# A decoder layer on one core: the norm weights loaded apart from the other vectors, with an earlier exp and a shorter warm-up

## The chip, the cores and the metric

The kernel runs on one core of a Trainium2 chip. The metric is the device time of one execution in microseconds (us). The engines are TensorE (PE; its weight loads are shown apart as PEld), VectorE (DVE), ScalarE (ACT), GpSimd (POOL) and SyncE (SP), which here issues most of the DMA transfers. Each engine works through its own instructions in order and waits on semaphores for the others.

## The reference

One layer (DEPTH 1) of a hybrid decoder, batch 1, 512 tokens with 16 learned meta tokens ahead of them (528 positions), model width 1024, all float32:

```python
def rmsnorm(x, w):
    xf = xf * lax.rsqrt(jnp.mean(xf * xf, axis=-1, keepdims=True) + EPS)
    return xf.astype(x.dtype) * w

h = jnp.concatenate([meta, x], axis=1)
u = rmsnorm(h, mix_norm_w[i])
proj = u @ w_in[i]                 # u_pool, z, xbc, dt_raw, gates
...
y_pool = pool_mixer(u_pool, ...) @ w_pool_up[i]
y_ssd = mamba2_branch(z, xbc, dt_raw, conv_w, conv_b, dt_bias, a_log, ...) @ w_ssd_out[i]
h = h + (gate_pool * y_pool + gate_ssd * y_ssd) @ w_o[i]
v = rmsnorm(h, mlp_norm_w[i])
hid = jax.nn.relu(v @ w_ff1[i])
h = h + (hid * hid) @ w_ff2[i]
out = rmsnorm(h, final_norm_w)
```

Only the start matters here: x is scaled by mix_norm_w and multiplied with columns of w_in. The division by the root mean square is done later, on the products, since it is one factor per token. dt = softplus(dt_raw + dt_bias) and a = -exp(a_log) feed the state-space branch.

## The kernel before, in words

Every float32 product is made of three matmuls on operands split into a high and a low part: ScalarE rounds the operand to the array's format (xh, whi), VectorE subtracts to get the rest (xl, wlo), and TensorE sums high by high, low by high and high by low. The model width is the contraction, in eight slices of 128 (k = 0 to 7). x arrives transposed, one slice a transfer (xt), 128 partitions by 528 tokens.

The start works as follows.

- Constants: an identity, ones in two formats (ones_f, and ones_r for the matmuls), eps. A table vs of 128 by 234 holds all small vectors of the layer, one column each: columns 0 to 7 are the norm weights (V_MIX), further ones are biases, the convolution's taps, dt_bias and a_log. It is loaded in one transfer on ScalarE's queue.
- Warm-up: WARM matmuls of ones_r by ones_r into a bank that is overwritten later (line 195).
- For each slice k, x_split makes xh and xl (lines 202 and 203), scaled by the norm weight of the slice; block_split makes whi and wlo of the weights (lines 79 and 80); bc_step(k) multiplies both weight blocks wB and wC with the slice (lines 148, 149 and 151, twelve matmuls a slice, into px). The weights of the first two blocks are loaded in parts: two quarters, and a half at k = 4.
- The square of each slice is taken on ScalarE (lines 231 and 234) and summed on VectorE into q (line 235).
- After slices 3 and 7, dt_step multiplies x with the 32 columns of dt (wdt, line 211, into pdt). Then pdt is copied (dtp, line 253) and gathered by small matmuls (pdv, line 257); q is summed over partitions (pn, line 274), which gives the norm factor rsb; dt's softplus and running sum follow (lines 307 to 341), with ea = exp(a_log) from line 312.

After that come the projections of the first group, seven further groups, the pool branch, the merge and the MLP.

The order on each engine is not the order of the code: a scheduler that plans with its own costs sets it before the run, and an instruction may move ahead of others of its engine. Hardware DMA semaphores are taken in turn from eight, so a DMA also waits for the one eight places before it. The line numbers in the profile of before are those of the old kernel.

Of the kernel before, what the change touches and what calls it, by code (L numbers as in the profile page):

```python
# [9 lines left out]
F32 = mybir.dt.float32  # L10
F32R = mybir.dt.float32r
AF = mybir.ActivationFunctionType
ALU = mybir.AluOpType

P = 128
# [5 lines left out]
NK = D // P  # L21
# [13 lines left out]
V_MIX, V_BG, V_PS, V_CW, V_CB, V_DS, V_SN, V_MN, V_DTB, V_AL = (  # L35
    0, 8, 24, 32, 160, 192, 208, 224, 232, 233)
# [6 lines left out]
MERGE = (0, 4, 1, 5, 2, 6, 3, 7)  # L43

WO_ORDER = [(q, i) for q in ("b11", "b12", "b22") for i in range(2)]
WARM = 9


@with_exitstack
def kernel(ctx: ExitStack, tc, xT, x, w, vec, fnw, out):  # L50
    nc = tc.nc
    act, dve, pe, pool = nc.scalar, nc.vector, nc.tensor, nc.gpsimd

    const = ctx.enter_context(tc.tile_pool(name="const", bufs=1, side="left"))
# [8 lines left out]
    def block_tiles():  # L63
        b = nblk[0]
        nblk[0] += 1
        return (b, wp.tile([P, 1024], F32, tag="raw", name=f"raw{b}", bufs=3),
                wp.tile([P, 1024], F32R, tag="whi", name=f"whi{b}"),
                wp.tile([P, 1024], F32R, tag="wlo", name=f"wlo{b}"))

    def block_load(t, c):  # L70
        nc.sync.dma_start(t[1][:, c], w[t[0], :, c])

    def block_part(t, c):
        block_load(t, c)
        block_split(t, c)

    def block_split(t, c):
        b, raw, hi, lo = t
        act.copy(hi[:, c], raw[:, c])  # L79
        dve.tensor_tensor(lo[:, c], raw[:, c], hi[:, c].bitcast(F32), op=ALU.subtract)  # L80
# [21 lines left out]
    make_identity(nc, ident)  # L102
    ones_r = const.tile([P, P], F32R, name="ones_r")
    ones_f = const.tile([P, P], F32, name="ones_f")
    dve.memset(ones_f, 1.0)
    dve.tensor_copy(ones_r, ones_f)
    tri = const.tile([P, P], F32, name="tri")
    pool.affine_select(out=tri, in_=ones_f, compare_op=ALU.is_ge, fill=0.0, base=0,
                       pattern=[[1, P]], channel_multiplier=-1)
# [2 lines left out]
    dve.tensor_copy(sel[:, 1, :], ident[:, NM - 1 : NM].to_broadcast([P, P]))  # L112
    eps = const.tile([P, 1], F32, name="eps")
    dve.memset(eps, EPS)
    vs = const.tile([P, V_N], F32, name="vs")
    nc.scalar.dma_start(vs, vec)

    def col(off, i, n=P):
        return vs[:n, off + i : off + i + 1]
# [24 lines left out]
    def proj_step(outs, k, wblk, rhs):  # L144

        wh, wl = (t[:, k * P : (k + 1) * P] for t in wblk)
        for o, c in outs:
            pe.matmul(o, wh, rhs[0][k][:, c], start=k == 0, stop=False)  # L148
            pe.matmul(o, wh, rhs[1][k][:, c], start=False, stop=False)  # L149
        for o, c in outs:  # L150
            pe.matmul(o, wl, rhs[0][k][:, c], start=False, stop=k == NK - 1)  # L151
# [16 lines left out]
    pre = pre_stack.enter_context(tc.tile_pool(name="pre", bufs=1, side="right"))  # L168
    xt = [pre.tile([P, L], F32, name=f"xt{k}") for k in range(NK)]

    xh = [pre.tile([P, 64 + SEQ], F32R, name=f"xh{k}")[:, 64 - NM :] for k in range(NK)]
    xl = [pre.tile([P, 64 + SEQ], F32R, name=f"xl{k}")[:, 64 - NM :] for k in range(NK)]
    pre.tile([P, 24], F32, name="x_pad")
    rsb = pre.tile([P, L], F32, name="rsb")
    q = pre.tile([P, L], F32, name="q")
    X, U = (xh, xl), (uh, ul)
    H = HEADS

# [7 lines left out]
    nblk[0] += 1  # L186
    wdt = pre.tile([P, NK, H], F32, name="wdt")
    wB, wC = block_tiles(), block_tiles()
    e32 = pre.tile([P, 2 * H], F32, name="e32")[:, :H]
    dve.tensor_tensor(e32, ident[:, :H], ident[:, H : 2 * H], op=ALU.add)  # L190
    for c in (2, 3):
        dve.tensor_tensor(e32, e32, ident[:, c * H : (c + 1) * H], op=ALU.add)

    for n in range(WARM):
        pe.matmul(pdt[1].rearrange("p (a b) -> p a b", a=4), ones_r,
                  ones_r.unsqueeze(1).to_broadcast([P, 4, P]), start=True, stop=True)

    def x_load(k):
        nc.sync.dma_start(xt[k], xT[:, k, :])

    def x_split(k):
        act.activation(xh[k], xt[k], AF.Copy, scale=col(V_MIX, k))
        dve.scalar_tensor_tensor(xl[k], xt[k], col(V_MIX, k), xh[k].bitcast(F32),
                                 op0=ALU.mult, op1=ALU.subtract)

    def dt_step(kb):

        for i, run in enumerate(HF):
            for c in range(4):
                k = kb + c  # L210
                pe.matmul(pdt[i][c * H : (c + 1) * H, :HALF], wdt[:, k, :], xt[k][:, run],
                          start=kb == 0, stop=kb == 4, skip_group_check=True)

    def bc_step(k):
        proj_step(runsB, k, wB[2:], X)
        proj_step(runsC, k, wC[2:], X)

    x_load(0)
    x_split(0)
    for t in (wB, wC):  # L220
        block_part(t, slice(0, 256))
    x_load(1)
    bc_step(0)
    x_split(1)
    x_load(2)
    for t in (wB, wC):
        block_part(t, slice(256, 512))
    bc_step(1)
    def square(k):
        if k == 0:  # L230
            act.activation(q, xt[k], AF.Square)
        else:
            s = pre.tile([P, L], F32, tag="sq", name=f"sq{k}", bufs=2)
            act.activation(s, xt[k], AF.Square)
            dve.tensor_tensor(q, q, s, op=ALU.add)

    for k in range(2, NK):
        if k > 2:
            x_load(k)
        x_split(k)  # L240
        if k == 2:
            nc.sync.dma_start(wdt.rearrange("p k h -> p (k h)"), w[b, :, : NK * H])
            dve.tensor_tensor(wdt, wdt, vs[:, V_MIX : V_MIX + NK].unsqueeze(2).to_broadcast([P, NK, H]), op=ALU.mult)
        if k == 4:
            for t in (wB, wC):
                block_part(t, slice(512, 1024))
        bc_step(k)
        if k % 4 == 3:
            dt_step(k - 3)
        square(k - 2)  # L250
# [506 lines left out]
    first = []  # L757
# [478 lines left out]
```

## Time and profile before

| | us |
|---|---|
| three runs, median | 1019.76 |
| lowest, highest | 1019.51, 1020.25 |
| the profiled execution, its own time | 1019.61 |
| its span, first to last instruction | 1017.6 |

| engine | busy us | share of the span |
|---|---|---|
| TensorE matmul | 1009.4 | 99% |
| TensorE weight load | 871.3 | 86% |
| VectorE | 739.5 | 73% |
| ScalarE | 550.4 | 54% |

A row of the timeline gives the start, the duration, the engine, the line, the operation, the tiles written and read, the shape and the count; in brackets stands the idle time of the engine ahead of it and what ended it. Matmuls are pipelined, so their durations overlap; their rate is read from one start to the next. Rows of neighbouring instructions of one kind are merged, with the count at the end. The profile leaves numbers out of names: wlo is any of the low weight blocks.

### The profile page before, as it was taken

What the parts mean: (1) busy time and instruction counts of PE and PEld (TensorE: products, weight loads), DVE (VectorE), ACT (ScalarE), POOL (GpSimd) and SP (SyncE); (2) the same over time, 40 slices, a digit from 0 to 9 for tenths busy, and PEclk for the clock granted to TensorE, in tenths of its full rate; (3) what the DMA queues carried; (4) which work ended last, traced back from release to release, by engine and by line L of the source; (5) the groups of instructions that cost most, each with busy time, mean ns of one, the idle gap of its engine ahead of it and who ended that gap; (6) DMA issues with size and microseconds to landing.
All of it is one profiled execution on the core that took longest, in us unless ns stands there. A gap on an engine that the chain in (4) does not pass through costs nothing.

```text
span 1017.6 us, 14071 instructions
## 1 busy us (share of the span) xinstructions
PE 1009.4 (99%) x5697; PEld 871.3 (86%) x5697; DVE 739.5 (73%) x988; ACT 550.4 (54%) x729; POOL 10.0 (1%) x24
## 2 busy tenths in 40 slices
PE   9999999999999999999999999999999999999997
PEld 8889989999879998988899888888888888888886
DVE  7988786777736577878765557986676686776866
ACT  8774959496727339473244233475445455454444
POOL 0000000000000000000000001000000000000000
PEclk9999999999999999999999999999999999999999
DMA  7242141515223230514532334133333324334112
GB/s 248 82 163 86 40 154 33 167 24 164 82 90 119 104 104 22 166 37 133 188 100 84 109 96 150 57 116 132 104 89 114 108 83 122 92 98 125 42 42 83
DMA packets 29712, 105.62 MB, mean 104 GB/s; under 512 B 3344, under 2 KB 4688, under 8 KB 28624
## 3 DMA queue, kind: packets, MB, share of 16 engines
q1 hardware_dynamic: 26928, 92.75, 29.0%
q0 software_dynamic: 2000, 11.08, 3.1%
q8 instruction: 45, 0.74, 0.3%
q10 hardware_dynamic: 720, 0.91, 0.2%
q14 instruction: 19, 0.16, 0.1%
HBM read 102.55 MB, written 2.16 MB: 103 GB/s over the span
## 4 chain that ended last, share of the span: by engine, by line
PE 98%; DVE 1%; DMA 0%; ACT 0%; SPq 0%; issue 0%; ACTq 0%
PE px L148 6%; PE px L151 6%; PE px L149 6%; PE pf L98 6%; PE pf L96 6%; PE pf L97 6%; PE alpha L985 3%; PE alpha L987 3%; PE alpha L986 3%; PE pz L149 3%; PE pz L148 3%; PE pz L151 3%; PE py L499 2%; PE pso L96 2%; PE pp L148 2%; PE pp L151 2%
## 5 line engine op out<-in xcount | busy, mean ns | idle before, releaser
L79 ACT CAST whi<-raw 128x1024 fp32r<-128x1024 f32 (+1 forms) x134 | 136.0, 1024 | 231.1 <-PE pf L97 58.7
L80 DVE TENSOR_TENSOR wlo<-raw,whi 128x1024 fp32r<-128x1024 f32 (+1 forms) x134 | 158.8, 1188 | 120.6 <-ACT whi L79 120.6
L148 PE MATMUL px<-uh,whi 128*128 128x264 f32 (+1 forms) x448 | 120.7, 290 | 0.7 <-DVE ct L363 0.7
L149 PE MATMUL px<-ul,whi 128*128 128x264 f32 (+1 forms) x448 | 117.9, 284 | 0.0
L96 PE MATMUL pf<-vh,whi 128*128 128x512 f32 x256 | 99.8, 390 | 0.0
L98 PE MATMUL pf<-vh,wlo 128*128 128x512 f32 x256 | 99.6, 389 | 0.0
L97 PE MATMUL pf<-vl,whi 128*128 128x512 f32 x256 | 99.6, 389 | 0.0
L151 PE MATMUL px<-uh,wlo 128*128 128x264 f32 (+1 forms) x448 | 91.0, 284 | 0.0
L148 PEld LDWEIGHTS px<-uh,whi 128*128 128x128 f32 x448 | 84.7, 189 | 2.7 <-issue 2.4
L149 PEld LDWEIGHTS px<-ul,whi 128*128 128x128 f32 x448 | 84.4, 188 | 0.4 <-issue 0.2
L151 PEld LDWEIGHTS px<-uh,wlo 128*128 128x128 f32 x448 | 68.9, 188 | 0.3 <-issue 0.2
L747 DVE TENSOR_TENSOR slo<-b,shi 128x1024 fp32r<-128x1024 f32 x35 | 42.7, 1219 | 31.6 <-ACT shi L746 31.6
L746 ACT CAST shi<-b 128x1024 fp32r<-128x1024 f32 x35 | 36.8, 1051 | 51.9 <-PE pf L97 36.5
L97 PEld LDWEIGHTS pf<-vl,whi 128*128 128x128 f32 x256 | 48.1, 188 | 10.0
L98 PEld LDWEIGHTS pf<-vh,wlo 128*128 128x128 f32 x256 | 48.0, 188 | 10.0
L96 PEld LDWEIGHTS pf<-vh,whi 128*128 128x128 f32 x256 | 48.1, 188 | 9.9
L985 PE MATMUL alpha<-shi,hh 128*128 128x512 f32 x140 | 54.6, 390 | 0.0
L986 PE MATMUL alpha<-slo,hh 128*128 128x512 f32 x140 | 54.5, 389 | 0.0
L987 PE MATMUL alpha<-shi,hl 128*128 128x512 f32 x140 | 54.5, 389 | 0.0
L812 DVE TENSOR_TENSOR ht<-ht,alpha 128x1024 f32<-128x1024 f32 x35 | 42.5, 1215 | 6.1 <-PE alpha L987 6.1
L148 PE MATMUL pz<-uh,whi 128*128 128x512 f32 x112 | 43.6, 390 | 0.0
L151 PE MATMUL pz<-uh,wlo 128*128 128x512 f32 x112 | 43.6, 390 | 0.0
(409 smaller groups left out, 2431.5 us busy)
## 6 DMA issues: line engine op xcount, KB each, us to landing
raw<-in_w SPq DMA_DIRECT2D x128, 512.0 KB, 3.6
b<-in_w SPq DMA_DIRECT2D x28, 512.0 KB, 3.6
abc<-acs_d POOLq DMA_DIRECT2D x8, 1024.0 KB, 6.9
wob<-in_w SPq DMA_DIRECT2D x8, 512.0 KB, 4.6
xt<-in_xT SPq DMA_DIRECT2D x8, 264.0 KB, 4.5
ht<-in_x POOLq DMA_DIRECT2D x4, 512.0 KB, 6.5
w<-in_w SPq DMA_DIRECT2D x4, 512.0 KB, 3.5
out_dram<-out SPq DMA_DIRECT2D x4, 320.0 KB, 2.4
```

Source lines behind the costliest of these rows:

```text
L79: act.copy(hi[:, c], raw[:, c])
L80: dve.tensor_tensor(lo[:, c], raw[:, c], hi[:, c].bitcast(F32), op=ALU.subtract)
L96: pe.matmul(ps, ah, bh, start=first, stop=False)
L97: pe.matmul(ps, ah, bl, start=False, stop=False)
L98: pe.matmul(ps, al, bh, start=False, stop=last)
L148: pe.matmul(o, wh, rhs[0][k][:, c], start=k == 0, stop=False)
L149: pe.matmul(o, wh, rhs[1][k][:, c], start=False, stop=False)
L151: pe.matmul(o, wl, rhs[0][k][:, c], start=False, stop=k == NK - 1)
L747: dve.tensor_tensor(lo, src, hi.bitcast(F32), op=ALU.subtract)
L985: pe.matmul(ps[t], a[0], wh[:, cs], start=f, stop=False, skip_group_check=True)
L986: pe.matmul(ps[t], a[0], wl[:, cs], start=False, stop=False, skip_group_check=True)
L987: pe.matmul(ps[t], a[1], wh[:, cs], start=False, stop=l, skip_group_check=True)
```

## The change

There are five edits. The eight norm weight columns get a tile of their own, vm, loaded on ScalarE's queue in place of the whole table; the x split and wdt's scaling read vm. The whole table vs is loaded from SP's queue, behind the weights' last parts at k = 4. An Exp of one column of eps is issued at the start, into a tile that nobody reads. ones_r is filled by a memset in place of a copy from ones_f. WARM goes from 9 to 8. (The width of e32's tile only keeps the addresses behind vm where they were.)

```diff
-WARM = 9
+WARM = 8
...
+    dve.memset(ones_r.bitcast(F32), 1.0)
     dve.memset(ones_f, 1.0)
-    dve.tensor_copy(ones_r, ones_f)
...
     dve.memset(eps, EPS)
+
+    act.activation(const.tile([P, 64], F32, name="first")[:, :1], eps, AF.Exp)
     vs = const.tile([P, V_N], F32, name="vs")
-    nc.scalar.dma_start(vs, vec)
...
+    vm = pre.tile([P, NK], F32, name="vm")
+    nc.scalar.dma_start(vm, vec[:, V_MIX : V_MIX + NK])
...
-    e32 = pre.tile([P, 2 * H], F32, name="e32")[:, :H]
+    e32 = pre.tile([P, 56], F32, name="e32")[:, :H]
...
     def x_split(k):
-        act.activation(xh[k], xt[k], AF.Copy, scale=col(V_MIX, k))
-        dve.scalar_tensor_tensor(xl[k], xt[k], col(V_MIX, k), xh[k].bitcast(F32),
+        act.activation(xh[k], xt[k], AF.Copy, scale=vm[:, k : k + 1])
+        dve.scalar_tensor_tensor(xl[k], xt[k], vm[:, k : k + 1], xh[k].bitcast(F32),
                                  op0=ALU.mult, op1=ALU.subtract)
...
-            dve.tensor_tensor(wdt, wdt, vs[:, V_MIX : V_MIX + NK].unsqueeze(2).to_broadcast([P, NK, H]), op=ALU.mult)
+            dve.tensor_tensor(wdt, wdt, vm.unsqueeze(2).to_broadcast([P, NK, H]), op=ALU.mult)
         if k == 4:
             for t in (wB, wC):
                 block_part(t, slice(512, 1024))
+            nc.sync.dma_start(vs, vec)
```

The scheduler's order changes with it on TensorE, VectorE and ScalarE, up to TensorE's 252nd entry of some 4,840; behind that the orders are the same. On VectorE the first sum into q moves from behind xl3 to ahead of xl2, and the second and third move from behind wlo and xl5 to ahead of xl4 and xl5. On ScalarE each square follows its split more closely, and ea moves from the first place to behind the fifth square. On TensorE one matmul of slices 1, 3 and 5 and some of the pdt matmuls move ahead of the first that needs xl, and pdv and pn move ahead of five matmuls of the next projection.

## The prediction

> **What bounds the kernel now.** I read the page's busy times and chain first, then busy time by stage, then the start instruction by instruction.
>
> ```profile
> PE 1009.4 (99%) x5697; PEld 871.3 (86%) x5697; DVE 739.5 (73%) x988; ACT 550.4 (54%) x729; POOL 10.0 (1%) x24
> PE 98%; DVE 1%; DMA 0%; ACT 0%; SPq 0%; issue 0%; ACTq 0%
> 3.00:4.00 1.00, 1.00 (x4) 0.81 (x3) 0.00 (x0) 0.00 (x0) 0.00 (x0) 1.00 1.09 362
> 8.00:20.00 12.00, 12.00 (x107) 10.88 (x111) 12.00 (x24) 11.86 (x21) 0.00 (x0) 1.00 0.74 272
> 50.00:1009.00 959.00, 958.06 (x5341) 826.74 (x5340) 692.83 (x892) 509.92 (x665) 6.88 (x13) 1.00 0.32 100
> ```
>
> The first two lines are from the page; the others are stretches (width, then busy PE, PEld, DVE, ACT, POOL, then clock, DMA share, GB/s). TensorE is the bound: from 50 to 1009 us it is busy 958.06 of 959.00 us. The instruction order of the changed kernel differs from the old one only in its first 252 TensorE entries (some 50 us) and is the same behind them. So what the change is worth is how much earlier TensorE leaves the start. There, between 8 and 20 us, VectorE (12.00 of 12.00) and ScalarE (11.86) are as full as TensorE: a second limit.
>
> The start, by the timeline (start, duration, engine):
>
> ```profile
> 1.50 4.21 PE L195 MATMUL pdt<-ones_r 128*128 128x512 f32 x9 [1.50 <-DVE ones_r L106]
> 5.57 0.89 PE L148 MATMUL px<-xh,whi 128*128 128x264 f32 x2
> 6.26 0.42 PE L149 MATMUL px<-xl,whi 128*128 128x264 f32 x1
> 6.48 0.34 PE L148 MATMUL px<-xh,whi 128*128 128x264 f32 x1
> 6.66 0.28 PE L149 MATMUL px<-xl,whi 128*128 128x264 f32 x1
> 6.78 0.40 PE L151 MATMUL px<-xh,wlo 128*128 128x264 f32 x2
> 7.62 0.28 PE L148 MATMUL px<-xh,whi 128*128 128x264 f32 x1
> 7.99 0.39 PE L149 MATMUL px<-xl,whi 128*128 128x264 f32 x1
> ```
>
> Nine warm-up matmuls fill 1.50 to 5.5 us, real work starts at 5.57, and TensorE then waits between 7.62 and 7.99 for the second slice's low half.
>
> ```profile
> 1.25 1.28 ACT L312 ACT_TABLE_LOAD   x1 [1.25 <-PEq L1228]
> 4.40 0.20 ACT L312 ACTIVATE ea<-vs 128x1 f32<-128x1 f32 x1 [1.86 <-DMA vs<-in_vec]
> 4.51 0.72 ACT L202 ACTIVATE xh<-xt,vs 128x528 fp32r<-128x528 f32 x1
> 5.13 0.69 ACT L79 CAST whi<-raw 128x256 fp32r<-128x256 f32 x2
> 6.40 1.44 ACT L202 ACTIVATE xh<-xt,vs 128x528 fp32r<-128x528 f32 x2 [0.57 <-DMA xt<-in_xT]
> vs<-in_vec ACTq DMA_DIRECT2D x1, 117.0 KB, 3.6
> xt<-in_xT SPq DMA_DIRECT2D x1, 264.0 KB, 3.3
> out_dram<-out ACTq DMA_DIRECT2D x4, 192.0 KB, 2.6
> SPq L242 <- DMA vs<-in_vec: 0.3, 1, 0.3
> ```
>
> The next to last three are DMA issues, with KB and us to landing (the xt row is that of slice 0 alone); the last is SP's wait ahead of wdt. Both loads are issued at 0.81: slice 0 is there at 0.81 + 3.3 = 4.11, vs at 0.81 + 3.6 = 4.41. ScalarE waits for vs, does ea, and only at 4.51 the first split. For slice 1 it waits for slice 1's own landing, 6.40.
>
> **The change part by part.**
>
> *The eight columns alone.* The first split no longer stands behind 117 KB and ea. vm carries 4 KB on ScalarE's queue. No load of 32 bytes per partition is in the trace; the nearest rows bound its landing: 2.6 us (the output stores) and 3.6 (vs itself), so 3.4 to 4.4 us. Slice 0 is needed too (4.11), so the first split starts between 4.11 and 4.42; I take 4.15, as few bytes go with it. The row behind it, whi, follows 0.62 later, and TensorE's first real matmul 0.44 after that: 5.2 instead of 5.57, a gain of 0.36 (bounds 0.09 to 0.40).
>
> The Trainium skill's page "DMA: Bandwidth & Descriptors", Specifications, speaks against this part: below 512 B per transfer it expects less than line rate. No run here has such a load; it is one of the rivals below.
>
> *Room on the DMA engines.* The row from 3 to 4 us shows them full (1.09). Without vs, 113 KB at that row's 362 GB/s, 0.31 us of traffic goes from ahead of slice 1. wdt's issue on SP also waited 0.3 us for vs; it will wait for vm, and less. Slice 1, and with it the split at 6.40, comes 0 to 0.35 earlier; I take 0.2.
>
> *vs behind the fourth weights.* It costs SP one issue (0.43 us) ahead of slices 5 to 7 and the next weights.
>
> ```profile
> 7.09 1.28 SPq L199 DMA_DIRECT2D xt<-in_xT  x3
> DMA to landing us min/median/max: 3.3/4.5/5.3
> 8.89 0.63 ACT L234 ACTIVATE sq<-xt 128x528 f32<-128x528 f32 x1
> 9.43 1.35 ACT L202 ACTIVATE xh<-xt,vs 128x528 fp32r<-128x528 f32 x2
> 10.68 0.60 ACT L79 CAST whi<-raw 128x512 fp32r<-128x512 f32 x1
> 0.90 0.17 DVE L105 MEMSET ones_f<- 128x128 f32 x1 [0.90 <-PEq L1228]
> ```
>
> vs goes out at about 7.09 and lands near 11.6 (the eight slices' median of 4.5), at worst at 12.4 (their slowest); slice 5, one issue later, at 12.8 at worst. ea now stands on ScalarE behind the fifth square, and xh5 behind ea. Adding up ScalarE's new order from 6.20 (xh 0.67, square 0.54, weight casts 0.35 and 0.60) gives ea at 12.9 and xh5 from 13.05 to 13.75: both loads are there. Next is late only if vs lands so late that xh5 ends after 14.4, where xl5 starts (below): beyond 13.5. vs's other readers come after 25 us. Cost: nothing.
>
> *Early exp.* The table load stands at 1.25 already; "first" keeps it there and takes 0.20 us of a 1.86 us wait. Nothing. ea's own 0.11 moves off the first split and is counted above.
>
> *Ones and warm-up.* The memset of ones_r at 0.90 takes the place of memset, memset and copy: TensorE's first warm-up moves from 1.50 to about 1.1. Eight at 0.43 end near 4.7, half a microsecond before real work. No engine waits for them; what they hold is the clock (a rival).
>
> *The order that follows.* The scheduler has put the squares' sums earlier on VectorE: one more sum (q) stands ahead of xl3, and one more again, net one, ahead of xl5. This is the price of the change.
>
> ```profile
> 5.26 0.77 DVE L203 SCALAR_TENSOR_TENSOR xl<-xt,vs,xh 128x528 fp32r<-128x528 f32 x1 [3.81 <-ACT xh L202]
> 7.17 1.47 DVE L203 SCALAR_TENSOR_TENSOR xl<-xt,vs,xh 128x528 fp32r<-128x528 f32 x2 [0.47 <-ACT xh L202]
> 10.18 0.77 DVE L203 SCALAR_TENSOR_TENSOR xl<-xt,vs,xh 128x528 fp32r<-128x528 f32 x1
> 10.87 0.70 DVE L235 TENSOR_TENSOR q<-q,sq 128x528 f32<-128x528 f32 x1
> 11.48 0.77 DVE L203 SCALAR_TENSOR_TENSOR xl<-xt,vs,xh 128x528 fp32r<-128x528 f32 x1
> 13.99 0.76 DVE L203 SCALAR_TENSOR_TENSOR xl<-xt,vs,xh 128x528 fp32r<-128x528 f32 x1
> 12.52 1.10 PE L211 MATMUL pdt<-xt,wdt 128*32 128x264 f32 x16
> 15.11 0.28 PE L148 MATMUL px<-xh,whi 128*128 128x264 f32 x1
> 15.22 0.28 PE L149 MATMUL px<-xl,whi 128*128 128x264 f32 x1
> 21.08 0.66 ACT L253 COPY dtp<-pdt 128x264 f32<-128x264 f32 x2
> 21.72 0.54 PE L257 MATMUL pdv<-dtp,e 128*32 128x128 f32 x16
> ```
>
> A sum costs 11.48 - 10.87 = 0.61. xl1 starts at 7.17 - 0.2 = 6.97 and ends at 7.74. xl3: 6.97 + 3.01 + 0.61 = 10.59, done at 11.36. xl5: 6.97 + 6.82 + 0.61 = 14.40, done at 15.16.
>
> TensorE against that, 0.12 a matmul (6.66 to 6.78) and twelve a slice: it takes up xl1 at 7.8 with ten matmuls of slice 1 left (9.0), slice 2 to 10.4, two of slice 3 and five of the small pdt matmuls, now moved ahead (about 0.15 each: eight, as sixteen records, from 12.5 to 13.6), to 11.4. xl3 has just come. The rest of slice 3 and three pdt end at 13.1, half a microsecond before the 13.6 of now. Slice 4 to 14.5; two matmuls and a pdt of slice 5 to 14.9; then it waits for xl5 until 15.2. There most of the lead is lost: now, slice 5 takes its low half at 15.22. What is left is that one matmul (0.12) and one pdt (0.15) are done ahead of the wait: **0.3 us**. With slice 1 no earlier it is 0.1, with 0.35 earlier 0.45.
>
> At 20 us the projection of dt (pdv) is moved ahead of some matmuls. pdt ends near 20.3, the copies dtp need 0.66, partly before that, and TensorE is at pdv after three matmuls, 20.7: a wait of 0.1 to 0.35 where now it is 0.1. That takes 0 to 0.25; I take 0.1. The rest follows in the old order.
>
> Sum: -0.2 us. The profiled execution took 1019.61 (span 1017.6 and 2.0 around it), 0.15 under the median of the three, 1019.76; it would become 1019.4, the median 1019.55, said as **1019.5**. The three times lie 0.74 apart, so this can't be told from no change; 0.2% (2.04 us) is about what a measurement of this kernel can tell.
>
> **The rivals.**
>
> *The clock comes later (slower).* The 264-column matmuls follow each other by 0.22 at 6.26 and by 0.12 from 6.66: the array runs at half speed until 6.6 us, 5.1 after its first matmul, though the clock column reads 1.00 (no record before then). If the new gap of 0.5 us between warm-up and work starts that count anew, half speed lasts from 5.2 to 10.3. Work worth 2.55 us is lost, against 0.5 now: 2.05 more. The earlier start gives back 0.36, the wait for xl1 0.3 and the lead that xl5 would have eaten another 0.4: 1.0 slower, **1020.8**. It decides once half speed lasts beyond 8.3 us; up to there those 1.06 hide it. For it: the warm-up is shorter and a gap is new. Against: the old stretch had gaps too (5.57 to 6.26 holds two matmuls of 0.22) and the clock still came. Chance 0.1.
>
> The Trainium skill's "TensorE: Matmul & The Clock Gate", Part 1, says that the gate opens after a busy window of about 3.4 us whose phase is free, so the same kernel warms at different times. The trace's 5.1 us from the first matmul agrees with a first window only half filled; by that rule the delay is one more window, an estimate of 1.7 us lost before waits absorb any.
>
> *Nothing moves.* Slice 1 lands at 6.40 as before, and xl5 and pdv eat the rest: **1019.75**. For it: the wait at 6.40 is for slice 1 itself, which the change doesn't touch. Chance 0.25.
>
> *All of the lead stays.* Slice 1 is 0.35 earlier, the sums turn out not to hold xl5, and TensorE keeps its 0.36, the 0.37 of waiting from 7.62 to 7.99 and the 0.1 at pdv: **1018.9**. Against it: VectorE's 12.00 of 12.00. Chance 0.13.
>
> *The small rows land late.* Later than vs did (4.41) costs nothing until the first low half delays the second: VectorE idles 0.47 ahead of 7.17. So it decides from 4.9 on; landing at 6.0 would give 1.1 later, **1020.8**. Chance 0.05.
>
> **How the numbers follow.** Forecast 0.45 (its own range 1019.2 to 1019.8, by the bounds above); the four rivals 0.53; 0.02 for the unseen. From 1018.9, the third rival, to 1020.4, inside the slower ones, at most 2 in 10 is out. None of the cases reaches 2.04 us: for that the clock or the small load would have to cost twice the price above. I give slower 0.05, faster 0.03, same 0.92.
>
> **What would show it.** In the new trace: the first real matmul near 5.2; the split of slice 1 at 6.1 to 6.3; ea near 12.6 without a wait; TensorE waiting for xl near 15; the 264-column spacing falling to 0.12 between 5 and 8 us. Wrong would be a xh behind vm later than 4.5, half speed after 8.3, or differences past 60 us.

## The result: 1.6 us slower, and the profile after

| | before | after |
|---|---|---|
| runs on one chip, side by side | 22 | 22 |
| median us | 1019.89 | 1021.46 |
| lowest, highest us | 1019.51, 1020.77 | 1021.17, 1022.03 |
| the profiled execution, its own time | 1019.61 | 1021.39 |
| its span | 1017.6 | 1019.6 |

The ratio after to before is 1.0015, with a 95% interval of 1.0009 to 1.0021. The changed kernel is 1.57 us slower: less than the 0.2% that the prediction took as measurable, but the interval leaves no room for the forecast gain. The time fell outside the predicted range (1018.9 to 1020.4).

The page and two stretches of the changed kernel, in the same form as in the prediction:

```profile
PE 1011.1 (99%) x5696; PEld 871.6 (85%) x5696; DVE 739.6 (73%) x988; ACT 550.7 (54%) x730; POOL 10.0 (1%) x24
8.00:20.00 12.00, 11.84 (x93) 9.86 (x93) 11.90 (x24) 10.78 (x19) 0.00 (x0) 1.00 0.78 286
50.00:1009.00 959.00, 958.02 (x5340) 826.71 (x5340) 693.61 (x894) 511.05 (x663) 7.14 (x14) 1.00 0.31 100
```

The long middle is as it was (958.02 of 959.00 us busy, 958.06 before). TensorE has 1.7 us more of work in all (1011.1 for 1009.4) with no more matmuls, and between 8 and 20 us it counts 93 matmuls where it had 107. Something in the start became more expensive for TensorE itself; its waits there add only 0.16 us of idle time.

TensorE's start in the changed kernel, chosen rows of the timeline (start, duration, line, tiles, shape, count):

```profile
1.12 3.78 PE L198 MATMUL pdt<-ones_r 128*128 128x512 f32 x8 [1.12 <-DVE ones_r L105]
5.00 0.59 PE L149 MATMUL px<-xh,whi 128*128 128x264 f32 x1
6.99 0.38 PE L150 MATMUL px<-xl,whi 128*128 128x258 f32 x1
7.20 0.29 PE L149 MATMUL px<-xh,whi 128*128 128x258 f32 x1
7.33 0.28 PE L150 MATMUL px<-xl,whi 128*128 128x258 f32 x1
8.25 0.39 PE L150 MATMUL px<-xl,whi 128*128 128x264 f32 x1 [0.16 <-DVE xl L206]
11.34 1.08 PE L214 MATMUL pdt<-xt,wdt 128*32 128x264 f32 x10
13.76 0.65 PE L214 MATMUL pdt<-xt,wdt 128*32 128x264 f32 x6
16.21 0.63 PE L214 MATMUL pdt<-xt,wdt 128*32 128x264 f32 x2
16.78 0.39 PE L150 MATMUL px<-xl,whi 128*128 128x264 f32 x1
21.09 1.09 PE L214 MATMUL pdt<-xt,wdt 128*32 128x264 f32 x14
```

Real work begins at 5.00 instead of 5.57. But the dt matmuls, each of which leaves two records, now stand in four pieces of five, three, one and seven, where they stood in two groups of eight (x16 each). The piece of one takes 0.63 us, the piece of three 0.65, the piece of seven 1.09: as much as a group of eight took (1.10). The same 32 records, summed over the first 24 us by operation and shape (before, then after; the column behind the bar is busy us):

```profile
L211 PE MATMUL pdt<-xt,wdt 128*32 128x264 f32 x32 | 2.2, 392 | 0.0
L214 PE MATMUL pdt<-xt,wdt 128*32 128x264 f32 x32 | 3.4, 395 | 0.0
```

That is 1.2 us of new TensorE time. Where it falls is seen at the first matmul of slice 2, of slice 4 and of slice 6, before and then after:

```profile
9.43 0.28 PE L148 MATMUL px<-xh,whi 128*128 128x264 f32 x1
13.55 0.39 PE L148 MATMUL px<-xh,whi 128*128 128x264 f32 x1
16.54 0.28 PE L148 MATMUL px<-xh,whi 128*128 128x264 f32 x1
```

```profile
9.57 0.28 PE L149 MATMUL px<-xh,whi 128*128 128x264 f32 x1
14.33 0.39 PE L149 MATMUL px<-xh,whi 128*128 128x264 f32 x1
18.09 0.28 PE L149 MATMUL px<-xh,whi 128*128 128x264 f32 x1
```

At slice 2 the changed kernel is 0.14 us late, although slice 1's low half was taken 0.26 later (8.25 for 7.99): one matmul more now stands ahead of that wait. The pieces of five and three make it 0.78 at slice 4, the piece of one makes it 1.55 at slice 6, and there it stays (the first matmul behind the second dt group stands at 22.11 for 20.56). So from start to start the pieces cost 1.4 us, a little more than their 1.2 of busy time.

The end of the kernel, before and after: ScalarE's last work, and SyncE's closing wait for the output stores (us in total, times, longest):

```profile
1013.56 0.61 ACT L1013 ACTIVATE out<-out,rt 128x384 f32<-128x384 f32 x1 [0.23 <-DVE rt L1012]
SPq L1232 <- DMA out_dram<-out: 1.8, 2, 1.5
```

```profile
1015.07 0.62 ACT L1017 ACTIVATE out<-out,rt 128x384 f32<-128x384 f32 x1 [0.23 <-DVE rt L1016]
SPq L1236 <- DMA out_dram<-out: 2.2, 1, 2.2
```

The last work of the engines is 1.51 us later (1015.07 for 1013.56), but the span is 2.0 us longer. From the start of that last instruction to the end of the span it is 4.04 us before and 4.53 after. So about half a microsecond is lost behind all computation, where the closing wait reads 2.2 us once instead of 1.8 in two.

### The profile page after: what moved, and what is told of

It reads as the page before. It is cut to its first block, busy times and chain, and to the rows that moved or that the text cites. A ratio compares the mean times of both kernels' runs of the same rounds, so it can differ in the third digit from the quotient of the medians.

```text
span 1019.6 us, 14072 instructions
## 1 busy us (share of the span) xinstructions
PE 1011.1 (99%) x5696; PEld 871.6 (85%) x5696; DVE 739.6 (73%) x988; ACT 550.7 (54%) x730; POOL 10.0 (1%) x24
## 4 chain that ended last, share of the span: by engine, by line
PE 98%; DVE 1%; DMA 0%; ACT 0%; SPq 0%; issue 0%; ACTq 0%
PE px L149 6%; PE px L150 6%; PE px L152 6%; PE pf L96 6%; PE pf L98 6%; PE pf L97 6%; PE alpha L989 3%; PE alpha L991 3%; PE alpha L990 3%; PE pz L152 3%; PE pz L149 3%; PE pz L150 3%; PE py L503 2%; PE pso L96 2%; PE pp L149 2%; PE pp L152 2%
```

## The experiments

Every kernel was run 11 times beside the kernel before (33 runs, medians 1019.75, 1019.71 and 1019.92 in the three groups of four). An interval of these ratios is about 0.0009, or 0.9 us, to either side. Single steps of half a microsecond are therefore read from the traces, and the medians have to agree with them. The changed kernel was not run beside e1 to e12: a difference from its 1021.46 compares two groups of runs. "Last work" is the start of that last ScalarE instruction; "tail" is from there to the end of the span.

| kernel | median us | ratio, interval | last work us | tail us |
|---|---|---|---|---|
| before | | | 1013.56 | 4.04 |
| after | 1021.46 | 1.0015 (1.0009 to 1.0021) | 1015.07 | 4.53 |
| e1_no_exp | 1020.85 | 1.0011 (1.0001 to 1.0020) | 1014.53 | 4.57 |
| e2_exp_alone | 1020.75 | 1.0009 (1.0001 to 1.0018) | 1014.74 | 4.06 |
| e3_grouped | 1020.54 | 1.0007 (0.9998 to 1.0015) | 1014.20 | 4.50 |
| e4_split | 1021.05 | 1.0012 (1.0003 to 1.0021) | 1015.32 | 4.08 |
| e5_pinned | 1020.89 | 1.0012 (1.0003 to 1.0021) | 1014.48 | 4.52 |
| e6_pinned_warm9 | 1020.91 | 1.0013 (1.0004 to 1.0021) | 1014.49 | 4.51 |
| e7_pinned_oldload | 1020.18 | 1.0006 (0.9997 to 1.0015) | 1014.26 | 4.14 |
| e8_warm8 | 1019.62 | 1.0000 (0.9991 to 1.0009) | 1014.12 | 4.08 |
| e9_lane | 1020.42 | 1.0005 (0.9996 to 1.0013) | 1013.63 | 4.57 |
| e10_one_store | 1020.89 | 1.0010 (1.0001 to 1.0019) | 1014.79 | 4.11 |
| e11_all_mended | 1020.57 | 1.0006 (0.9997 to 1.0015) | 1014.25 | 4.05 |
| e12_x1_act | 1019.29 | 0.9995 (0.9986 to 1.0004) | 1012.92 | 4.08 |

The last work of one profiled execution carries that execution's own start. e8_warm8 has the median of the kernel before to within 0.1 us, but its profiled execution is 0.57 us above that median, and its last work is 0.56 later than before. In it slice 1's split started at 6.73 and not at 6.40, and TensorE waited for the low halves of slices 1 and 3:

```profile
8.32 0.39 PE L149 MATMUL px<-xl,whi 128*128 128x264 f32 x1 [0.41 <-DVE xl L203]
11.66 0.39 PE L149 MATMUL px<-xl,whi 128*128 128x264 f32 x1 [0.18 <-DVE xl L203]
```

So differences of half a microsecond in this column count only where the rows of the start account for them. The tail does not have this scatter.

**Which edit breaks the groups?** The changed kernel without the early exp, and the kernel before with it alone:

```diff
# e1_no_exp: after
-    act.activation(const.tile([P, 64], F32, name="first")[:, :1], eps, AF.Exp)
# e2_exp_alone: before
+    act.activation(const.tile([P, 64], F32, name="first")[:, :1], eps, AF.Exp)
```

> The change without the early exp (vm, vs behind the weights, ones by memset, 8 warm-ups stay). Its TensorE order is the old one: the dt matmuls stand in two whole groups of eight. Split groups as the cause: the 1.1 us that the dt matmuls cost more in the changed kernel is gone, 1020.3 or less; their time in the trace falls from 3.2 to 2.1 us. Clock gate as the cause (fewer warm-ups, a gap): the loss stays, 1021.4. Sums of squares ahead on VectorE as the cause: gone too, 1020 or less.

> The kernel before with the early exp and nothing else: nine warm-ups and the old loads, but the order changes: dt matmuls in pieces of 5, 3 and 8, the sums of squares earlier on VectorE. Split groups: one piece more than before costs 0.55, 1020.4. Clock gate: no change, 1019.9. Sums of squares: most of the loss is here, 1021 or more, with TensorE waiting for a low half.

The start of e2_exp_alone on TensorE, then ScalarE's and TensorE's start in e1_no_exp:

```profile
11.20 1.08 PE L213 MATMUL pdt<-xt,wdt 128*32 128x264 f32 x10
13.61 0.65 PE L213 MATMUL pdt<-xt,wdt 128*32 128x264 f32 x6
20.17 1.10 PE L213 MATMUL pdt<-xt,wdt 128*32 128x264 f32 x16
```

```profile
3.71 1.28 ACT L203 ACT_TABLE_LOAD   x1 [3.71 <-DMA xt<-in_xT]
5.00 0.73 ACT L203 ACTIVATE xh<-xt,vm 128x528 fp32r<-128x528 f32 x1
6.09 0.89 PE L147 MATMUL px<-xh,whi 128*128 128x264 f32 x2 [1.18 <-ACT whi L79]
```

The exp alone makes the scheduler break the first group into five and three, and the kernel is 1.0 us slower than before (1020.75 for 1019.75). Its order breaks a second group as well: the gathering matmuls pdv stand in pieces of one and seven (at 21.40 and 22.53, 0.41 and 0.47 us, for 0.54 in one piece before), so the 1.0 is not the price of five and three alone (1020.4 was expected for those). Without the exp the groups stay whole, and yet e1_no_exp missed the 1020.3 expected of it (1020.85). For now the table load, which used to run at 1.25 us ahead of ea, sits behind the wait for the first slice, and real work starts at 6.09 instead of 5.00. Its profiled execution lost time in another way too:

```profile
9.17 0.36 PE L148 MATMUL px<-xl,whi 128*128 128x264 f32 x1
9.36 0.29 PE L147 MATMUL px<-xh,whi 128*128 128x264 f32 x1
```

Its matmuls follow each other by 0.22 us up to 9.17 and by 0.12 from 9.36 on, and TensorE takes slice 1's low half at 9.17, though VectorE had it done at 8.33 (started at 7.56, 0.77 long). How much of the 1.1 us is the late table load and how much the late full speed isn't shown. What is shown: the price of the exp is not its 0.20 us on ScalarE but the order that the scheduler then plans, and leaving it out puts the table load in the way.

**Do the broken groups cost what the trace says?** Mended in the changed kernel, and made by hand in the kernel before (the pieces there are five and three, one and seven):

```diff
# e3_grouped: after, dt matmuls held in the order of the code
-                pe.matmul(pdt[i][c * H : (c + 1) * H, :HALF], ...)
+                tc.keep_in_program_order(pe.matmul(pdt[i][c * H : (c + 1) * H, :HALF], ...))
# e4_split: before, dt_step called by parts and held there
         if k == 3:
+            dt_step(0, DT[:5])        # ahead of bc_step(3); the other three behind it
         if k == 5:
+            dt_step(4, DT[:1])        # ahead of bc_step(5); the other seven behind bc_step(7)
```

> The changed kernel with each dt matmul held behind what stands ahead of it in the code, so that they are two whole groups of eight again; exp, loads, ones and 8 warm-ups as changed, and the sums of squares still early. Split groups: 1.1 less than the changed kernel, 1020.3. Clock gate: 1021.4. Sums of squares: 1021.4, with the waits for the low half.

> The kernel before with its dt matmuls cut as in the changed one (5 and 3 around slice 3, 1 and 7 around slice 5); nine warm-ups, loads, ScalarE's and VectorE's order as before. Split groups: 1.1 more than before, 1021.0, and 3.2 us of dt matmuls in place of 2.1. Clock gate and sums of squares: no change, 1019.9.

The dt matmuls in e3_grouped, then in e4_split:

```profile
L214 PE MATMUL pdt<-xt,wdt 128*32 128x264 f32 x32 | 2.2, 392 | 0.0
```

```profile
L211 PE MATMUL pdt<-xt,wdt 128*32 128x264 f32 x32 | 3.4, 395 | 0.0
```

Mending takes 0.92 us off the changed kernel (1021.46 to 1020.54; measured against the kernel before in each group, the loss falls from 1.57 to 0.79); breaking puts 1.30 on the kernel before (1019.75 to 1021.05). Both are of the size of the 1.2 of the rows. That mending gives back less has a reason in e3_grouped's trace. With the pieces gone, TensorE is early at slice 3's low half and waits for it:

```profile
10.98 0.40 PE L149 MATMUL px<-xh,whi 128*128 128x264 f32 x2
11.78 0.39 PE L150 MATMUL px<-xl,whi 128*128 128x264 f32 x1 [0.41 <-DVE xl L206]
```

Two matmuls at 0.12 would have ended their turn at 11.22, so 0.56 us passes here; in the changed kernel five dt matmuls fill this place. The broken groups are the largest part of the result.

**The sums, the warm-up and the clock.** e5_pinned holds the sums of squares, too, in the old order; e6_pinned_warm9 is that with nine warm-ups; e7_pinned_oldload is e5_pinned with the vectors loaded as before; e8_warm8 is the kernel before with eight warm-ups.

```diff
# e5_pinned: e3_grouped
-            dve.tensor_tensor(q, q, s, op=ALU.add)
+            tc.keep_in_program_order(dve.tensor_tensor(q, q, s, op=ALU.add))
# e6_pinned_warm9: e5_pinned
-WARM = 8
+WARM = 9
# e7_pinned_oldload: e5_pinned
+    nc.scalar.dma_start(vs, vec)         # as before: no vm, and no load of vs at k = 4
# e8_warm8: before
-WARM = 9
+WARM = 8
```

> The changed kernel with the dt matmuls in two whole groups (as in the run before it) and, besides, each sum of squares on VectorE held behind the low half that stands ahead of it in the code, so that the sums stand where they stood in the kernel before; loads, exp, ones and 8 warm-ups as changed. Split groups and early sums as the two causes: the wait of 0.4 us for slice 3's low half goes and slice 3 ends 0.6 earlier; 1019.9, level with before. Clock gate as the rest of the loss: still 1020.5.

> The run above with nine warm-ups in place of eight, which end some 5.1 us after the start, at the first real matmul. Clock gate: no gap, so half speed ends earlier on average; faster than the run above by 0.3 or more, and less spread. Groups and sums: within 0.1 of the run above.

> The same pinned order, 8 warm-ups, early exp and ones by memset, but the norm weights come with the whole table of vectors on ScalarE's queue as in the kernel before. If the early start that vm brings is worth something: 0.3 slower than the run with vm. If slice 1's landing decides: level with it, the first real matmul near 5.5.

> The kernel before with eight warm-ups in place of nine and nothing else; every engine's order is the old one. The warm-up ends 0.4 us ahead of real work. Clock gate: half speed lasts longer, 0.3 to 1.0 slower than before. Groups and sums: level with before.

Holding the sums gained nothing in the median (1020.89 against 1020.54, where 1019.9 was expected). The traces show two effects that cancel. The pause ahead of slice 3's low half shrinks from 0.56 to 0.31 us (in e5_pinned the two matmuls ahead of it start at 11.09 and it is taken at 11.64), so the early sums do cost TensorE about a quarter of a microsecond once the groups are whole. But in e5_pinned, and in e6 and e7 too, pdv stands in pieces of one and seven. From the first matmul behind the second dt group to the last work it is 993.4 to 993.5 us in these three, and 992.9 to 993.1 in all kernels whose pdv is whole. Eight or nine warm-ups make no difference, neither with the new load (1020.89 and 1020.91) nor in the kernel before (1019.62 and 1019.71), so the shorter warm-up is not the cause. Only going back to the old load took something off (0.71 us, e5_pinned to e7_pinned_oldload, where slower or level was expected), and the table shows where most of it lies: of the two, the one with the new load has a tail of 4.52 and the other of 4.14. In these first eight kernels every one with the new load has the long tail and none of the others.

**What is the half microsecond at the end?** In these programs the hardware loads and stores take one of eight semaphores in turn. The kernel before issues 192 of them, a whole number of rounds, so its last store takes the last of the eight. The changed kernel issues 193 (vm is one more), so its last store takes the first. SyncE's closing waits go through the eight in order. One kernel adds a load that nothing uses, in the middle of the kernel before; the other has one store less in the changed kernel:

```diff
# e9_lane: before
+    nc.sync.dma_start(hp_.tile([P, NK], F32, name="extra"), vec[:, :NK])
# e10_one_store: after, rows of block 0 stored in one piece
+        if t:
             nc.scalar.dma_start(out[t * P : (t + 1) * P, :384], o[:, :384])
...
-        nc.sync.dma_start(out[t * P : (t + 1) * P, 384:], o[:, 384:])
+        a = 384 if t else 0
+        nc.sync.dma_start(out[t * P : (t + 1) * P, a:], o[:, a:])
```

> The kernel before with one 4-KB load more on SyncE's queue, issued in the middle of the kernel into a tile that nothing reads. Hardware loads and stores take one of eight semaphores in turn; the kernel before issues 192 of them, so its last store takes the last of the eight, and the changed kernel issues 193, so its last store takes the first. At the end SyncE waits for the eight in order. Theory (the extra load moves the last store to the first of the eight, and the seven waits behind it run only when it has landed): TensorE's shift against the kernel before stays within 0.6 us of none from the start to the end, as from run to run, and SyncE's closing wait reads 2.2 us once instead of 1.8 us in two, and the span is 0.4 to 0.5 us longer than TensorE's shift explains. Rival (the 0.45 us at the end belongs to the new loads of norm weights themselves): the closing wait stays at 1.8 us in two and the span moves as TensorE does.

> The changed kernel with the first of the four blocks of output rows stored in one piece instead of two, so that it issues 192 hardware loads and stores again; its start is untouched. Theory: SyncE's closing wait goes back to 1.8 us in two, the time falls by 0.45 us against the changed kernel, from 1021.46 to about 1021.0, and TensorE's shift against the kernel before stays at 1.5 us. Rival (the end depends on something else of the change): closing wait 2.2 us, time as the changed kernel's.

The closing wait in e9_lane, then in e10_one_store:

```profile
SPq L1233 <- DMA out_dram<-out: 2.2, 1, 2.2
```

```profile
SPq L1238 <- DMA out_dram<-out: 1.8, 2, 1.5
```

The idle extra load turns the short tail into the long one (4.57) with the last work within 0.07 us of the kernel before, and the store saved turns it back (4.11) with the start still broken. The medians move by +0.50 and -0.57. Over all fourteen kernels, the six with 193 have tails of 4.50 to 4.57 us and the eight with 192 of 4.04 to 4.14, whatever else they hold. That SyncE steps through seven further waits behind the last landing is the reading of the program's order; the trace shows the one wait of 2.2, not the steps. Shown is that one hardware DMA more or less makes the difference; no kernel here had another count than 192 or 193, so the round of eight itself isn't tested.

**Everything mended, and one step further.** e11_all_mended is e5_pinned with the single store of e10_one_store. e12_x1_act also issues the second slice from ScalarE's queue, behind vm:

```diff
# e12_x1_act: e11_all_mended
-        nc.sync.dma_start(xt[k], xT[:, k, :])
+        (nc.scalar if k == 1 else nc.sync).dma_start(xt[k], xT[:, k, :])
```

> The changed kernel with the dt matmuls held in two whole groups, the sums of squares held in the order of the code, and the first block of output stored in one piece: the broken groups and the closing wait are both taken away, the early load of norm weights, the early exp and the warm-up stay. Theory (these two are what the change cost): 1020.4, the earlier 1020.89 less 0.45, and within 0.1% of the kernel before; it would beat it only if the 0.5 us that TensorE's first matmul is earlier lasted past the second slice. Rival (the new loads cost something of their own in the first 10 us): 1020.8 to 1021.0.

> As the kernel with everything mended, and the second slice of x is issued from ScalarE's queue behind the eight columns of norm weights, near 1.3 us, instead of from SyncE's queue at 2.2 us. Theory (the early first matmul is lost because the second slice lands no earlier): the second slice's split starts at 6.0 instead of 6.7, its first matmul at about 7.0 instead of 7.7, TensorE is up to 0.7 us earlier there, and the time is 1019.7 to 1020.2, which could be under the kernel before. Rival (the traffic of the first two microseconds sets the landing, not the issue): the first slice or the weights land later by as much, the first matmul comes at 5.5 or later, and the time is 1020.4 or more.

The gathering matmuls pdv in e11_all_mended, then the start of e12_x1_act (ScalarE's queue and splits, TensorE):

```profile
21.07 0.41 PE L262 MATMUL pdv<-dtp,e 128*32 128x128 f32 x2
22.10 0.47 PE L262 MATMUL pdv<-dtp,e 128*32 128x128 f32 x14
```

```profile
1.25 0.45 ACTq L202 DMA_DIRECT2D xt<-in_xT  x1
5.97 1.36 ACT L205 ACTIVATE xh<-xt,vm 128x528 fp32r<-128x528 f32 x2
6.12 0.38 PE L149 MATMUL px<-xh,whi 128*128 128x258 f32 x1 [0.22 <-ACT whi L79]
7.54 0.29 PE L149 MATMUL px<-xh,whi 128*128 128x264 f32 x1
7.66 0.29 PE L150 MATMUL px<-xl,whi 128*128 128x264 f32 x1
20.61 0.48 PE L262 MATMUL pdv<-dtp,e 128*32 128x128 f32 x16
```

e11_all_mended is 0.9 us under the changed kernel, not the 1.4 to 1.5 that the groups and the tail came to one by one: as in e5_pinned, with the sums held the scheduler broke another packed group, pdv, into one and seven (0.41 + 0.47 for 0.54 in the kernel before), and from the first matmul behind the second dt group to the last work it is 993.6 us. The mechanism just removed came back at another place. In e12_x1_act pdv is whole again, with the sums still held, and that stretch is 992.9. Both sides of its expectation were half right: the second slice's split starts at 5.97 as the theory said, but the weights land later as the rival said (TensorE waits for whi, and is at slice 1 only at 7.54). What it gains at the start is that TensorE waits for no low half any more (7.54 and 7.66 follow each other at full rate); the first matmul behind the second dt group comes 0.57 us earlier than in e11_all_mended. The whole pdv behind it gives the rest. It measures 1019.29, the lowest of all and 0.6 us under the kernel before (1019.92 beside it); the interval of the ratio, 0.9986 to 1.0004, includes no change. That it beats the kernel before is not shown.

## Why the prediction was wrong, point by point

- *TensorE is the bound, and only the start differs:* the first half holds (958.02 of 959.00). "What the change is worth is how much earlier TensorE leaves the start" left out the tail: one more hardware DMA costs 0.5 us behind all work. The text ahead of the prediction says that eight semaphores are taken in turn, but only for waits on issue; the prediction never asks what that does at the end.
- *The price of a dt matmul, "about 0.15 each":* this is the step that failed. It divided a group of eight (1.1 us) by eight and carried the quotient to pieces of five, three and one. Measured are 1.08, 0.65 and 0.63, and 1.09 for the seven left: that fits a price by rounds of up to four that run side by side (the code gives each of four dt matmuls its own 32 columns). With these prices in the prediction's own timeline, TensorE reaches slice 5's low half at 15.9 instead of 15.2, xl5 is there already, and the seven left cost as much as eight did: the forecast of -0.2 becomes about +0.6. The second mis-sized term is slice 1's landing, below, and the third is the tail that was left out.
- *The eight columns alone:* right in kind, and more than its bounds allowed. vm's 4 KB landed 3.1 us after issue and the first split began at 3.92 (predicted 4.15, bounds 4.11 to 4.42), so slice 0 too was there sooner than reckoned; the first real matmul stands at 5.00 (5.2), a gain of 0.57 where at most 0.40 was allowed. It bought nothing, since TensorE then stood at slice 1's low half.

```profile
2.54 0.20 ACT L116 ACTIVATE first<-eps 128x1 f32<-128x1 f32 x1
3.92 0.74 ACT L205 ACTIVATE xh<-xt,vm 128x528 fp32r<-128x528 f32 x1 [1.17 <-DMA vm<-in_vec]
6.66 0.74 ACT L205 ACTIVATE xh<-xt,vm 128x528 fp32r<-128x528 f32 x1 [0.87 <-DMA xt<-in_xT]
13.03 0.18 ACT L316 ACTIVATE ea<-vs 128x1 f32<-128x1 f32 x1
vs<-in_vec SPq DMA_DIRECT2D x1, 117.0 KB, 4.6
vm<-in_vec ACTq DMA_DIRECT2D x1, 4.0 KB, 3.1
```

- *Room on the DMA engines:* wrong by its sign here. Slice 1's split started at 6.66, not at 6.2, and TensorE came to slice 2 at 9.57, where the prediction had 9.0: another 0.6 us, which with the pieces makes about +1.2 and with the tail +1.7 for a measured 1.57. Over the profiled executions the spread is wider than any effect: 6.27 to 6.73 in the six kernels with the old load, 6.28 to 6.79 in the seven with the new one that issue slice 1 from SyncE. The freed 117 KB bought nothing that can be seen; issuing the slice earlier did (5.97 in e12_x1_act).
- *vs behind the fourth weights, ones:* right. ea ran at 13.03 (predicted 12.9) with no wait.
- *Early exp at no cost:* right for ScalarE (0.20 us of a wait), wrong for the kernel, since the scheduler's order hangs on it. The prediction had that order before it, and listed the pieces; only their price was wrong.
- *The sums and xl5:* a sum's size was right (0.6), the place not. TensorE came to slice 5's low half at 16.78, long after xl5, because the pieces had delayed it; it waited only 0.16 us in all for a low half (8.25). With the pieces mended the wait appears, at slice 3 (e3_grouped, above). Where one engine gets slower, another's lateness stops mattering.
- *The rivals:* half speed lasts until 7.2 us (from 6.99 to the next 0.21, from 7.20 to the next 0.13), below the 8.3 from which it would decide, and e5_pinned, e6_pinned_warm9 and e8_warm8 close the case for the number of warm-ups. The moment itself scatters: the spacing falls to 0.12 at 5.73 in e5_pinned and at 9.36 in e1_no_exp, where it came later than 8.3 and may have cost time. The Trainium skill's rule of a window with a free phase ("TensorE: Matmul & The Clock Gate", Part 1) agrees with this scatter, but in the changed kernel nothing hung on it. The small rows did not land late: 3.1 us against 3.6 for the whole table before. The rule of the Trainium skill's "DMA: Bandwidth & Descriptors", Specifications, that had spoken for this rival is one of rate; the trace shows no late landing from it. "Nothing moves" would have been nearer than the forecast. Neither rival on the slow side named the mechanism that decided; their place and sign were argued from waits, and the loss was in work.

The sum that the runs give: 1.2 us of broken groups and 0.5 us of tail make 1.7, against a measured 1.57. By undoing, 0.92 and 0.57 make 1.49; by adding to the kernel before, 1.30 and 0.50 make 1.80. Of these four only the 1.30 is clear of no change by its own interval; what speaks for the others is that the three sums agree and that the traces show the pieces and the tails. What is left over either way, 0.1 to 0.2 us, can't be told from nothing by these runs.

## What to carry to other kernels

Price small matmuls that share the array by the round, not by the piece: when a changed order cuts a group, count rounds of each fragment. Ask of any added or removed DMA what it does to the closing waits, and compare the tail behind the last work as a figure of its own. An edit that costs an engine nothing can still move a planner's order, so its price is that of the order; pinning one part of it can break the next.

## What the runs showed of the hardware that was not expected

Three dt matmuls of 32 columns cost hardly more than one, and five as much as eight (0.63 us for a piece of one, 0.65 for three, 1.08 for five, 1.10 for eight). The Trainium skill's "TensorE: Matmul & The Clock Gate", Part 3, says that tiles placed side by side in the array span the time of one plus about 4 ns for each further one. The trace agrees in kind (0.02 us for two more); that a fragment costs a whole round is the other side of that rule. A 4-KB load in rows of 32 bytes landed 3.1 us after issue at the start, where the 117 KB of vs had taken 3.6 before, and the same load in the middle of e9_lane took 1.6 (issues, KB, us to landing):

```profile
extra<-in_vec SPq DMA_DIRECT2D x1, 4.0 KB, 1.6
```

And that one unused load, in the middle of the kernel, made the tail 0.5 us longer (4.57 for 4.04); that the turn of the semaphores does it is the reading, not a row of the trace.
